# A two-layer decoder trunk: in the gated MLPs, the remainder of every second weight piece made by an accumulating transfer

## The chip, the cores and the metric

The kernel runs on one core of a Trainium2 chip, in one launch. Times are microseconds (us) on the device; the metric is the median of several runs. A separate execution was recorded by the hardware profiler, and all views quoted below come from it. The engines are called PE (TensorE; PEld is its weight load), DVE (VectorE), ACT (ScalarE), POOL (GpSimd) and SP (SyncE). SP issues the weight loads.

## The reference, cut to what matters

The input is a float32 residual stream of 256 tokens by 2048 features. Two layers follow. Each has a mixer (layer 0: gMLP beside HGRN2, layer 1: FoX attention) and then a gated MLP with a short causal convolution; the change concerns the MLP alone:

```
def conv_ffn(h, w_up, conv_w, conv_b, w_down):
    z = h @ w_up                                   # 2048 -> 2 * 5632
    zp = pad(z, two rows of zeros ahead)
    z = sum(conv_w[j] * zp[:, j:j + seq] for j in range(3)) + conv_b
    a, b = split(z, 2)
    return (silu(a) * b) @ w_down                  # 5632 -> 2048
...
x = x + conv_ffn(rms_norm(x, ffn_norm[l]), ...)
```

All weights are float32, and the products are wanted at nearly float32 precision.

## The kernel before, in words

**Layout.** The stream is kept feature-major: sixteen tiles `xT[m]` of 128 features by 256 tokens. A product with a weight matrix has the weights stationary in PE (128 x 128) and the tokens moving.

**Two-part products.** PE takes operands in a reduced form of float32 (`F32R`). To keep the precision, a value is split into a rounded part and the remainder. For activations, `split` puts the rounded part into columns 0 to 255 of a 128 x 512 tile and the remainder into columns 256 to 511. For weights, `weights(src, n)` loads a piece `w` (SP), lets ACT copy it to `wh` with rounding (L139), and lets DVE make the remainder `wl = w - wh` (L141).

**A projection.** `project` makes 128 output features from all input features. It takes its weights in two pieces: `chunks=(8, 8)`, two pieces of 128 x 1024 (512 KB each), in the up-projections, and `chunks=(6, 5)`, pieces of 128 x 768 (384 KB) and 128 x 640 (320 KB), in the down-projections. For each of the 16 or 11 input tiles there are two matmuls: `wh` against all 512 columns (L155) and `wl` against the first 256 (L157), both into one accumulator `pm`. That pair is called a pair below. `fold` (L187, L188) adds the two halves of the accumulator; `project_norm` then multiplies with the norm's factor R (L195); `add_x` (L264 to L266) adds the result of a down-projection to the stream.

**The MLP.** `ffn` handles the 44 hidden tiles in four groups of eleven. `up(g)` runs `conv` for the a and the b part of each tile: one up-projection, the convolution on ACT and DVE (L673 to L675), then silu, the product and the split into `hid`. `down(g)` runs sixteen down-projections over the group's eleven tiles. The order is up(0), up(1), down(0), up(2), down(1), up(3), down(2), down(3). In all, each layer's MLP has 88 up-projections and 64 down-projections, 88 x 16 + 64 x 11 = 2112 pairs of matmuls.

**Buffers and order.** Weight pieces come from two pools. `wp` lives for the whole kernel and has four buffers for `w`, three for `wh` and three for `wl`. A second pool, `fw`, is opened for each MLP (`deep["pool"]`) in memory that the mixer used before, and has four, two and two. `deep["turn"]` counts the pieces of an MLP: the first six come from `wp`, and from then on every second piece comes from `fw`. A framework plans the order of the instructions on each engine and sets all the waits; each engine then works through its own list in order. An instruction that fills a buffer waits until the last reader of the buffer's previous contents is done, so the number of buffers sets how far ACT, DVE and the loads may run ahead of PE.

**GpSimd** has almost nothing to do: one small load at the start and some additions in the first 30 us.

Of the kernel before, what the change touches and what calls it, by code (L numbers as in the profile page):

```python
# [7 lines left out]
F32 = mybir.dt.float32  # L8
F32R = mybir.dt.float32r
BF16 = mybir.dt.bfloat16  # L10
AF = mybir.ActivationFunctionType
ALU = mybir.AluOpType
AX = mybir.AxisListType

P = 128
# [7 lines left out]
GRP = 11  # L23
# [21 lines left out]
def tile_trunk(ctx: ExitStack, tc: tile.TileContext, x, pp_d, cst_d, mlev_d, msk_d,  # L45
               w_v, w_f, w_g, w_i, w_q, w_u, w_abo, w_cf, w_cqkv, w_cg, w_co, w_up, w_dn, spw_d, spb_d, out):
    nc = tc.nc
    V, SC, PE = nc.vector, nc.scalar, nc.tensor

    cp = ctx.enter_context(tc.tile_pool(name="cp", bufs=1))  # L50
    wp = ctx.enter_context(tc.tile_pool(name="wp", bufs=4))
# [7 lines left out]
    def nm(base):  # L59
        count[0] += 1  # L60
        return f"{base}_{count[0]}"
# [3 lines left out]
    for c0, n in ((0, 2), (2, 2), (4, 4), (8, 4), (12, 4)):  # L65
        t = cp.tile([P, n, S], F32, tag=f"x{c0}", name=f"x{c0}")
# [15 lines left out]
    def act(out_, in_, func, **kw):  # L82
        name = TABLE.get(func)
        if name is not None and name != epoch["set"]:
            ld = SC.preload_act_table_set(name)
            for o in epoch["ops"]:
                tc.add_manual_dep(ld.ins, o.ins.name, order, reason="table order")
            epoch.update(set=name, load=ld, ops=[ld])
        r = SC.activation(out_, in_, func, **kw)
        if name is not None:  # L90
            tc.add_manual_dep(r.ins, epoch["load"].ins.name, order, reason="table order")
            epoch["ops"].append(r)
        return r
# [14 lines left out]
    def tick():  # L108
        while queue and len(flight) < depth[0]:
            flight.append(queue.pop(0))  # L110
        for g in list(flight):
            if next(g, flight) is flight:
                flight.remove(g)
# [11 lines left out]
        while flight or queue:  # L125
            tick()

    deep = {"pool": None, "turn": 0}

    def weights(src, n):  # L130
        deep["turn"] += 1
        if deep["pool"] is not None and deep["turn"] > 6 and deep["turn"] % 2:
            pool, nw, ns = deep["pool"], 4, 2
        else:
            pool, nw, ns = wp, 4, 3
        w = pool.tile([P, n], F32, tag="w", name=nm("w"), bufs=nw)
        nc.sync.dma_start(w, src)
        wh = pool.tile([P, n], F32R, tag="wh", name=nm("wh"), bufs=ns)
        SC.activation(wh, w, AF.Copy)  # L139
        wl = pool.tile([P, n], F32R, tag="wl", name=nm("wl"), bufs=ns)  # L140
        V.tensor_tensor(wl, w, wh.bitcast(F32), ALU.subtract)  # L141
        return wh, wl

    def project(wsrc, acts, chunks=(8, 8), k0=0):
        ps = pm.tile([P, 512], F32, tag="pm", name=nm("pm"))
        nk = sum(chunks)
        done = 0
        for c in chunks:
            lo = (k0 + done) * P
            tick()  # L150
            wh, wl = weights(wsrc[:, lo:lo + c * P], c * P)
            for k in range(c):
                a = acts[done + k]
                first, last = done + k == 0, done + k == nk - 1
                PE.matmul(ps, wh[:, k * P:(k + 1) * P], a,  # L155
                          start=first, stop=False, skip_group_check=True)
                PE.matmul(ps[:, S:2 * S], wl[:, k * P:(k + 1) * P], a[:, 0:S],  # L157
                          start=False, stop=last, skip_group_check=True)
            done += c
        return ps  # L160
# [24 lines left out]
    def fold(ps):  # L185
        t = tp.tile([P, S], F32, tag="ev", name=nm("ev"), bufs=3)
        SC.activation(t, ps[:, S:2 * S], AF.Copy)  # L187
        V.tensor_tensor(t, ps[:, 0:S], t, ALU.add)  # L188
        return t

    def project_norm(wsrc, acts, R, out=None):
        t = fold(project(wsrc, acts))
        if out is None:
            out = t
        V.tensor_tensor(out, t, R, ALU.mult)  # L195
        return out

    def split(dst, src, gain=None):
        if gain is None:
            SC.activation(dst[:, 0:S], src, AF.Copy)  # L200
            V.tensor_tensor(dst[:, S:2 * S], src, dst[:, 0:S].bitcast(F32), ALU.subtract)
        else:
            SC.activation(dst[:, 0:S], src, AF.Copy, scale=gain)
            V.scalar_tensor_tensor(dst[:, S:2 * S], src, gain, dst[:, 0:S].bitcast(F32),  # L204
                                   ALU.mult, ALU.subtract)
# [56 lines left out]
    def add_x(m, ps):  # L262
        t = tp.tile([P, S], F32, tag="ev", name=nm("ev"), bufs=3)
        SC.activation(t, ps[:, S:2 * S], AF.Copy)  # L264
        V.tensor_tensor(xT[m], xT[m], ps[:, 0:S], ALU.add)
        V.tensor_tensor(xT[m], xT[m], t, ALU.add)  # L266

# [1 line left out]
    def mixer_ab(norm):  # L269
        es = ExitStack()  # L270
        hp = es.enter_context(tc.tile_pool(name="hp", bufs=1))
# [4 lines left out]
        def keep(n):  # L276
            return hp.tile([P, S], F32, tag="keep", name=nm(n), bufs=3 * NH)

        # gMLP's v, two groups of four heads with the tokens on the partitions
        gv, late = [], []  # L280

        def finish():
# [6 lines left out]
        for g in range(2):  # L289
            ps = project_tok(w_v[g], norm, feed=g == 0)  # L290
            v = hp.tile([P, 2, 512], F32, tag="tok", name=nm("gv"), bufs=2)
# [5 lines left out]
            else:  # L297
                drain()
                R, Rt = late
                for T in range(2):  # L300
                    act(v[:, T], ps[T], AF.Gelu, scale=Rt[:, T:T + 1])
        A = norm.a
# [18 lines left out]
        for g in range(2):  # L321
            for T in range(2):
                i = (2 * g + T) * 4
                j = hp.tile([P, 512], F32, tag="smk", name=nm("junk"), bufs=1)
# [28 lines left out]

        queue.append(mixes())

        # the lower bound, softmax over the first axis of gamma
        gam = pp[:, C_GAM:C_GAM + 3 * NH]
        gm = hp.tile([P, 4 * NH], F32, tag="gm", name="gm")
        mx, sm_, lb, omlb = (gm[:, i * NH:(i + 1) * NH] for i in range(4))
# [16 lines left out]
        for h in range(NH):  # L376
            z = project_norm(w_f[h], A, R)
            l = keep("lf")
            t = hp.tile([P, 2, S], F32, tag="two", name=nm("kq"), bufs=2 * NH)
# [101 lines left out]
        for h in range(NH):  # L481
            z = fold(project(w_q[h], A))
# [29 lines left out]
        for h in range(NH):  # L512
            z = hp.tile([P, S], F32, tag="zu", name=nm("zu"), bufs=5)
# [16 lines left out]
        for m in range(KT):  # L530
            add_x(m, project(w_abo[m], ks))
            nxt.feed(m)
        es.close()
        return nxt

# [1 line left out]
    def mixer_c(norm):  # L537
        es = ExitStack()
        hp = es.enter_context(tc.tile_pool(name="cpool", bufs=1))
# [112 lines left out]
        es.close()  # L652
        return nxt

# [1 line left out]
    def ffn(l, norm, last):  # L656
        es = ExitStack()
        hp = es.enter_context(tc.tile_pool(name="fp", bufs=1))
        deep.update(pool=es.enter_context(tc.tile_pool(name="fw", bufs=1)), turn=0)
        A = norm.a  # L660
        R = norm.finish()
        nxt = None if last else Norm(C_MIX + KT)

        def conv(j):
            z = project_norm(w_up[l, j], A, R)

            def w(i):
                c = C_CW + (l * 3 + i) * 2 * HT + j
                return pp[:, c:c + 1]

            cb = C_CB + l * 2 * HT + j
            c = hp.tile([P, S], F32, tag="conv", name=nm("conv"), bufs=4)
            SC.activation(c, z, AF.Identity, bias=pp[:, cb:cb + 1], scale=w(2))  # L673
            V.scalar_tensor_tensor(c[:, 1:], z[:, :S - 1], w(1), c[:, 1:], ALU.mult, ALU.add)  # L674
            V.scalar_tensor_tensor(c[:, 2:], z[:, :S - 2], w(0), c[:, 2:], ALU.mult, ALU.add)  # L675
            return c

        def up(g):
            hid = []
            for i in range(GRP):  # L680
                j = g * GRP + i
                a = conv(j)
                b = conv(HT + j)
                act(a, a, AF.Silu)
                V.tensor_tensor(a, a, b, ALU.mult)
                t = hp.tile([P, 512], F32R, tag="hid", name=nm("hid"), bufs=2 * GRP)
                split(t, a)
                hid.append(t)
            return hid

        def down(g, hid):
            for m in range(KT):
                add_x(m, project(w_dn[l, m], hid, chunks=(6, 5), k0=g * GRP))
                if g == HT // GRP - 1:
                    if last:
                        nc.sync.dma_start(out[:, m, :], xT[m])
                    else:
                        nxt.feed(m)

        hids = [up(0)]  # L700
        for g in range(HT // GRP):
            if g + 1 < HT // GRP:
                hids.append(up(g + 1))
            down(g, hids[g])
        deep["pool"] = None
        es.close()
        return nxt

    banks.update(px=3, pd=2)
    norm = mixer_ab(Norm(C_MIX))  # L710
    norm = ffn(0, norm, False)
    norm = mixer_c(norm)
    ffn(1, norm, True)


# [78 lines left out]
```

## Time and profile before

| | before |
|---|---|
| time, median of 3 runs | 2390.92 us |
| lowest and highest run | 2390.84 and 2404.64 us |
| span of the profiled execution | 2389.0 us |
| median minus span | 1.9 us |
| mean granted PE clock | 0.999 of full speed |
| PE / PEld busy | 2377.3 / 2060.0 us |
| DVE / ACT / POOL busy | 1756.3 / 1317.2 / 16.1 us |
| moved by DMA | 440.73 MB, mean 184 GB/s |
| first gated MLP | from about 429 to 1162 us |
| second gated MLP | from about 1640 us to the end |

The profiled execution's own time is its span, from the first to the last instruction, and what lies around it; the runs' median is 1.9 us above the span. A group of instructions is given as line, engine, operation, `out<-in` by the program's names, shapes and count, then busy time, mean nanoseconds of one, and the idle time of the engine just before, with what ended it. In the lists of waits, a row says who waited for whom, then the total in us, how often, and the longest. In windows, the columns are the length, the busy time of PE, PEld, DVE, ACT and POOL (with the number of instructions), the granted PE clock, the mean busy share of the 16 DMA engines, and GB/s. For DMA issues, KB is the size of one and the last number is the median time from issue to landing. PE's matmuls are pipelined and their ends are modelled, so a full PE is not a PE at its peak.

### The profile page before, as it was taken

The numbers are of one execution on the slowest core, as the hardware profiler recorded it, in microseconds if no ns is written. First come the engines' busy times: TensorE is split into PE (matmuls) and PEld (weight loads), VectorE is DVE, ScalarE is ACT, GpSimd is POOL, SyncE is SP. The second block draws the span as 40 slices with busy tenths as digits, with TensorE's granted clock in tenths as the row PEclk, the third lists the DMA queues.
The fourth block names the chain that finished last, engine by engine and source line by source line (L and its number), as shares of the span: only waits on it lengthen the run. The fifth ranks groups of instructions, "written<-read, shape, count | busy, mean of one in ns | idle before, by whom it ended". The sixth has DMA issues, their size and how long they took to land.

```text
span 2389.0 us, 35728 instructions
## 1 busy us (share of the span) xinstructions
PE 2377.3 (100%) x13198; PEld 2060.0 (86%) x13198; DVE 1756.3 (74%) x2954; ACT 1317.2 (55%) x2169; POOL 16.1 (1%) x20
## 2 busy tenths in 40 slices
PE   8999999999999999999999999999999999999999
PEld 7888888888888888888888888888888888888888
DVE  6767786888867877777756666777777767767765
ACT  6655565655555555555545455556555555545543
POOL 2000000000000000000000000000000000000000
PEclk9999999999999999999999999999999999999999
DMA  7544455755566566566655555557555565565564
GB/s 265 177 159 135 141 184 187 241 190 191 169 187 213 177 173 222 176 170 188 200 175 177 175 159 167 188 192 237 186 186 186 156 220 186 152 220 185 153 188 145
DMA packets 133869, 440.73 MB, mean 184 GB/s; under 512 B 14880, under 2 KB 16944, under 8 KB 133440
## 3 DMA queue, kind: packets, MB, share of 16 engines
q1 hardware_dynamic: 132224, 433.40, 57.5%
q10 hardware_dynamic: 1440, 5.01, 0.6%
q8 instruction: 104, 1.70, 0.3%
q14 instruction: 69, 0.57, 0.1%
q0 software_dynamic: 32, 0.05, 0.0%
HBM read 436.29 MB, written 2.11 MB: 184 GB/s over the span
## 4 chain that ended last, share of the span: by engine, by line
PE 97%; DMA 1%; DVE 1%; issue 0%; ACT 0%; SPq 0%; DVEq 0%; ACTq 0%
PE pm L155 53%; PE pm L157 27%; PE pm L177 5%; PE pm L178 5%; PE pm L176 5%; PE px L439 1%; DVE wl L141 0%; DMA w<-in_w_v 0%; DMA mst<-in_mlev 0%; PE pd L411 0%; DMA w<-in_w_up 0%; PE pd L412 0%; PE px L612 0%; PE px L576 0%; PE px L583 0%
## 5 line engine op out<-in xcount | busy, mean ns | idle before, releaser
L141 DVE TENSOR_TENSOR wl<-w,wh 128x1024 fp32r<-128x1024 f32 (+3 forms) x900 | 1015.7, 1129 | 538.1 <-ACT wh L139 534.3
L139 ACT ACTIVATE wh<-w 128x1024 fp32r<-128x1024 f32 (+3 forms) x900 | 883.4, 982 | 952.2 <-PE pm L155 653.4
L155 PE MATMUL pm<-a,wh 128*128 128x512 f32 x3600 | 1266.0, 396 | 0.0
L157 PE MATMUL pm<-a,wl 128*128 128x256 f32 x3600 | 1010.5, 281 | 0.5 <-DVE wl L141 0.5
L155 PEld LDWEIGHTS pm<-a,wh 128*128 128x128 f32 x3600 | 675.0, 187 | 157.1 <-DVE a L204 0.8
L157 PEld LDWEIGHTS pm<-a,wl 128*128 128x128 f32 x3600 | 680.3, 189 | 1.6 <-DVE wl L141 0.8
L155 PE MATMUL pm<-hid,wh 128*128 128x512 f32 x1408 | 493.1, 395 | 0.0
L157 PE MATMUL pm<-hid,wl 128*128 128x256 f32 x1408 | 394.8, 280 | 0.0
L155 PEld LDWEIGHTS pm<-hid,wh 128*128 128x128 f32 x1408 | 263.9, 187 | 61.9
L157 PEld LDWEIGHTS pm<-hid,wl 128*128 128x128 f32 x1408 | 266.0, 189 | 0.0
L176 PE MATMUL pm<-wh,a 128*128 128x512 f32 x512 | 204.0, 400 | 2.1 <-ACT wh L139 2.1
L177 PE MATMUL pm<-wl,a 128*128 128x512 f32 x512 | 202.0, 395 | 3.5 <-DVE wl L141 3.5
L178 PE MATMUL pm<-wh,a 128*128 128x512 f32 x512 | 201.6, 394 | 0.0
L177 PEld LDWEIGHTS pm<-wl,a 128*128 128x128 f32 x512 | 97.0, 189 | 25.3 <-DVE wl L141 5.9
L176 PEld LDWEIGHTS pm<-wh,a 128*128 128x128 f32 x512 | 97.2, 190 | 21.7 <-ACT wh L139 2.4
L178 PEld LDWEIGHTS pm<-wh,a 128*128 128x128 f32 x512 | 96.7, 189 | 20.2
L673 ACT ACTIVATE conv<-ev,pp 128x256 f32<-128x256 f32 x176 | 103.4, 587 | 16.2 <-DVE ev L195 16.2
L188 DVE TENSOR_TENSOR ev<-pm,ev 128x256 f32<-128x256 f32 x225 | 93.8, 417 | 3.4 <-ACT ev L187 3.4
L674 DVE SCALAR_TENSOR_TENSOR conv<-ev,pp,conv 128x255 f32<-128x255 f32 x176 | 84.2, 478 | 8.1 <-ACT conv L673 8.1
L675 DVE SCALAR_TENSOR_TENSOR conv<-ev,pp,conv 128x254 f32<-128x254 f32 x176 | 85.1, 483 | 6.2
L155 PE MATMUL pm<-yc,wh 128*128 128x512 f32 x256 | 88.8, 391 | 0.0
L195 DVE TENSOR_TENSOR ev<-ev,R 128x256 f32<-128x256 f32 x184 | 78.3, 425 | 6.1
(181 smaller groups left out, 1602.7 us busy)
## 6 DMA issues: line engine op xcount, KB each, us to landing
w<-in_w_up SPq DMA_DIRECT2D x352, 512.0 KB, 4.3
w<-in_w_dn SPq DMA_DIRECT2D x128, 384.0 KB, 3.2
w<-in_w_cqkv SPq DMA_DIRECT2D x96, 512.0 KB, 3.6
w<-in_w_dn SPq DMA_DIRECT2D x128, 320.0 KB, 3.3
w<-in_w_abo SPq DMA_DIRECT2D x32, 512.0 KB, 4.3
w<-in_w_cg SPq DMA_DIRECT2D x32, 512.0 KB, 3.9
w<-in_w_co SPq DMA_DIRECT2D x32, 512.0 KB, 3.5
w<-in_w_f SPq DMA_DIRECT2D x16, 512.0 KB, 3.6
```

The lines of the kernel that those rows point to most:

```text
L139: SC.activation(wh, w, AF.Copy)
L141: V.tensor_tensor(wl, w, wh.bitcast(F32), ALU.subtract)
L155: PE.matmul(ps, wh[:, k * P:(k + 1) * P], a, start=first, stop=False, skip_group_check=True)
L157: PE.matmul(ps[:, S:2 * S], wl[:, k * P:(k + 1) * P], a[:, 0:S], start=False, stop=last, skip_group_check=True)
L176: PE.matmul(ps[T], ah, h, start=k + i == 0, stop=False)
L177: PE.matmul(ps[T], ah, l, start=False, stop=False)
L178: PE.matmul(ps[T], al, h, start=False, stop=k + i == KT - 1)
L188: V.tensor_tensor(t, ps[:, 0:S], t, ALU.add)
L195: V.tensor_tensor(out, t, R, ALU.mult)
L673: SC.activation(c, z, AF.Identity, bias=pp[:, cb:cb + 1], scale=w(2))
L674: V.scalar_tensor_tensor(c[:, 1:], z[:, :S - 1], w(1), c[:, 1:], ALU.mult, ALU.add)
L675: V.scalar_tensor_tensor(c[:, 2:], z[:, :S - 2], w(0), c[:, 2:], ALU.mult, ALU.add)
```

## The change

A second way to make the two parts of a weight piece, `weights_acc`, is added. It loads `w` as before. ACT writes the negated, rounded copy of `w` straight into `wl`. GpSimd then issues a transfer from `w` to `wl` that adds to what is there, so that `wl` becomes `w` minus the rounded `w`. A second copy on ACT makes `wh` as before. DVE has no part in it. `project` gets an argument `acc`, the offsets of the pieces that go this way: the second piece of each up-projection (offset 8) and the second piece of each down-projection (offset 6). All pieces of the new kind come from the pool `fw`, now with four buffers for `w`, four for `wl` and three for `wh`, from the first projection of an MLP on; all others come from `wp`. The counter `turn` is gone. The mixers use `weights` as before.

```diff
-    deep = {"pool": None, "turn": 0}
+    deep = {"pool": None}
 
     def weights(src, n):
-        deep["turn"] += 1
-        if deep["pool"] is not None and deep["turn"] > 6 and deep["turn"] % 2:
-            pool, nw, ns = deep["pool"], 4, 2
-        else:
-            pool, nw, ns = wp, 4, 3
+        pool, nw, ns = wp, 4, 3
         w = pool.tile([P, n], F32, tag="w", name=nm("w"), bufs=nw)
         nc.sync.dma_start(w, src)
         wh = pool.tile([P, n], F32R, tag="wh", name=nm("wh"), bufs=ns)
...
+    def weights_acc(src, n):
+        pool = deep["pool"]
+        w = pool.tile([P, n], F32, tag="w", name=nm("w"), bufs=4)
+        nc.sync.dma_start(w, src)
+        wl = pool.tile([P, n], F32R, tag="wl", name=nm("wl"), bufs=4)
+        SC.activation(wl, w, AF.Copy, scale=-1.0)
+        nc.gpsimd.dma_start(wl, w, accum_op=ALU.add)
+        wh = pool.tile([P, n], F32R, tag="wh", name=nm("wh"), bufs=3)
+        SC.activation(wh, w, AF.Copy)
+        return wh, wl
+
-    def project(wsrc, acts, chunks=(8, 8), k0=0):
+    def project(wsrc, acts, chunks=(8, 8), k0=0, acc=()):
...
-            wh, wl = weights(wsrc[:, lo:lo + c * P], c * P)
+            wh, wl = (weights_acc if done in acc else weights)(wsrc[:, lo:lo + c * P], c * P)
...
-    def project_norm(wsrc, acts, R, out=None):
-        t = fold(project(wsrc, acts))
+    def project_norm(wsrc, acts, R, out=None, acc=()):
+        t = fold(project(wsrc, acts, acc=acc))
...
-        deep.update(pool=es.enter_context(tc.tile_pool(name="fw", bufs=1)), turn=0)
+        deep.update(pool=es.enter_context(tc.tile_pool(name="fw", bufs=1)))
...
-            z = project_norm(w_up[l, j], A, R)
+            z = project_norm(w_up[l, j], A, R, acc=(8,))
...
-                add_x(m, project(w_dn[l, m], hid, chunks=(6, 5), k0=g * GRP))
+                add_x(m, project(w_dn[l, m], hid, chunks=(6, 5), k0=g * GRP, acc=(6,)))
```

## The prediction

> **What bounds the kernel now.** The profile page comes first: the engines' shares and the chain that ended last.
>
> ```profile
> span 2389.0 us, 35728 instructions
> ...
> PE 2377.3 (100%) x13198; PEld 2060.0 (86%) x13198; DVE 1756.3 (74%) x2954; ACT 1317.2 (55%) x2169; POOL 16.1 (1%) x20
> ...
> q1 hardware_dynamic: 132224, 433.40, 57.5%
> ...
> PE 97%; DMA 1%; DVE 1%; issue 0%; ACT 0%; SPq 0%; DVEq 0%; ACTq 0%
> ```
>
> TensorE is busy for 2377.3 of 2389.0 us, so all idle time of PE together is 11.7 us, and the chain is 97% PE. VectorE's 74% and the DMA queue's 57.5% lie beside it. The waits say whether VectorE, which the change relieves, ever holds PE up.
>
> ```profile
> ACT wh L139 <- PE pm L155: 653.4, 573, 3.1
> DVE wl L141 <- ACT wh L139: 534.3, 752, 3.5
> ...
> PEld pm L177 <- DVE wl L141: 5.9, 6, 2.5
> ...
> PE pm L177 <- DVE wl L141: 3.5, 4, 2.1
> ...
> PEld pm L157 <- DVE wl L141: 0.8, 1, 0.8
> ```
>
> It hardly does. L177 is in the token-major projections of the mixers, which the change leaves alone; L157, the matmul on `wl` that the gated MLPs use, has 0.8 us in one wait. The long waits run the other way: ScalarE waits for PE to give a `wh` buffer back, 653.4 us in 573 waits, 1.14 us each. ScalarE and VectorE are ahead of PE and stop because the buffers are full. Last, the two gated MLPs as windows (columns: PE, weight load, DVE, ACT, POOL busy, clock, DMA share, GB/s).
>
> ```profile
> 429.00:1162.00 733.00, 733.00 (x4228) 645.99 (x4228) 566.97 (x909) 414.84 (x669) 0.00 (x0) 1.00 0.61 189
> 1640.00:2389.00 749.00, 744.33 (x4210) 644.73 (x4208) 553.67 (x876) 399.65 (x634) 0.00 (x0) 1.00 0.59 184
> ```
>
> These two stages are 1482 us of the span. In the first PE is never idle, in the second for 4.67 us. So VectorE's relief has at most 4.67 us to give here; the question is only whether what replaces its work stays below PE.
>
> **The change part by part.** Per layer there are 88 up-projections of two 1024-wide pieces and 64 down-projections of a 768- and a 640-wide piece. The second piece of each takes the new way: 88 + 64 = 152 pieces per layer, 304 in all. Their prices by shape, first gated MLP:
>
> ```profile
> L141 DVE TENSOR_TENSOR wl<-w,wh 128x1024 fp32r<-128x1024 f32 x176 | 215.5, 1225 | 86.2 <-ACT wh L139 85.8
> ...
> L139 ACT ACTIVATE wh<-w 128x1024 fp32r<-128x1024 f32 x177 | 187.7, 1062 | 195.1 <-PE pm L155 191.8 <-DMA w<-in_w_up 1.5 <-issue 1.4
> ...
> L141 DVE TENSOR_TENSOR wl<-w,wh 128x640 fp32r<-128x640 f32 x64 | 52.7, 824 | 31.7 <-ACT wh L139 31.7
> ...
> L139 ACT ACTIVATE wh<-w 128x640 fp32r<-128x640 f32 x64 | 47.3, 739 | 42.5 <-PE pm L155 41.0
> ```
>
> *Removed:* 88 subtractions of 1.225 us and 64 of 0.824 us, 107.8 + 52.7 = 160.5 us of VectorE per layer, 567 down to 406. All of it lay beside PE: gain 0, at most the 4.67 us above.
>
> *Added on ScalarE:* the negated copy, a second ACTIVATE of the same shape: 88 x 1.062 + 64 x 0.739 = 93.5 + 47.3 = 140.8 us per layer, 414.8 up to 555.6 of 733 us (76%). It is hidden by the idle time in which ScalarE now waits for PE. If that cover were gone, it would cost at most those 140.8 us per layer. The new copy waits for its `w` and for one of four `wl` buffers, and behind it in ScalarE's order stand the `wh` copies of the next pieces and the copy L187 that empties the accumulators; for these PE waits. The buffers reach about three projections ahead, so I take 0.
>
> *Added on GpSimd:* 304 transfers. The trace has one DMA issue by POOL, and POOL does nothing else in these stages:
>
> ```profile
> 1.24 0.68 POOL L74 DMA_DIRECT2D pp<-in_pp  x1 [0.79 <-POOLq L783]
> ...
> pp<-in_pp POOLq DMA_DIRECT2D x1, 50.0 KB, 6.3
> ```
>
> At 0.68 us per issue 88 + 64 issues are 103 us per layer: POOL is no bound, even at double that. In its order each transfer waits for the negated copy, with only later transfers queued behind it, all for later pieces. Landing takes 4.3 us in the median for a load of 512 KB (row below), and a transfer of twice the work some 9 us. `wl` has four buffers in every second piece, so a transfer may start three projections ahead: PE takes 733 us for 152 projections, 4.8 us each, so some 14 us. The delay of one transfer is hidden; what counts is how much all of them take of the DMA engines.
>
> *Added on the 16 DMA engines, the main term.* A transfer takes 512 KB (up) or 320 KB (down) of `w` and adds it onto the `wl` of that size: 88 x 0.524 + 64 x 0.328 = 67.1 MB per layer for one pass. The trace shows no accumulating transfer and none from SBUF to SBUF; the nearest rows are the weight loads.
>
> ```profile
> 426.00:429.00 3.00, 3.00 (x17) 2.33 (x16) 1.96 (x3) 1.53 (x4) 0.00 (x0) 1.00 1.00 362
> 429.00:432.00 3.00, 3.00 (x18) 2.66 (x18) 2.05 (x4) 2.59 (x5) 0.00 (x0) 1.00 1.01 380
> 435.00:438.00 3.00, 3.00 (x19) 2.63 (x18) 2.96 (x4) 2.87 (x5) 0.00 (x0) 1.00 1.01 377
> 444.00:447.00 3.00, 3.00 (x19) 2.63 (x19) 2.55 (x5) 1.89 (x5) 0.00 (x0) 1.00 1.00 384
> ...
> w<-in_w_up SPq DMA_DIRECT2D x352, 512.0 KB, 4.3
> ```
>
> Two prices follow. On average over a stage: 0.61 x 733 us for 189 GB/s x 733 us = 138.5 MB, 3.23 us of all 16 engines per MB (second stage 0.59 x 749 / 137.8 = 3.21). In bursts, with all 16 engines full: mean of 362, 380, 377 and 384 is 376 GB/s, 2.66 us per MB. The difference is that a packet's time has waiting in it, which overlaps with the next packet's once the queues are full.
>
> Bounds for the transfers: at best one pass at the burst price, 67.1 x 2.66 = 178 us per layer; at worst three passes (read `w`, read `wl`, write `wl`, nothing overlapped) at the average price, 201.3 x 3.23 = 650 us. Less than nothing is excluded, since all the loads stay. I take two passes, since both operands must be read while writing can run beside it, at the average price, since reading back what will be written is a less even stream than a load: 134.2 x 3.23 = 433 us (second layer 134.2 x 3.21 = 431). It is close to the middle of the ends, 414. The loads then run with full queues, at the burst price: 138.5 x 2.66 = 368 us (137.8 x 2.66 = 367). Sums: 801 us of DMA against 733 us of PE in the first MLP, 798 against 749 in the second. The DMA engines become the bound: +68 and +49, together +117 us. VectorE, ScalarE and PE then wait; what is late is `wl` of the second piece, and through the `w` buffers the loads.
>
> The Trainium skill, Collectives: The Full Stack, "The bandwidth ceiling: the fold count and why AG ≠ RS ≠ AR", says that an addition made by the DMA engines costs nothing for itself, but reads two sources over one ring and so runs at half the rate of a copy: the two passes I count. No run here shows it yet. DMA: Bandwidth & Descriptors, "Issuing engines are not separate DMA queues", speaks against the change as well: a transfer from GpSimd runs on the same 16 DMA engines as the loads from SyncE.
>
> *Moved: the start of each MLP.* Now the first six pieces come from `wp`, already free; after the change the second piece of the first projection needs the MLP's own pool, whose memory the mixer held.
>
> ```profile
> 408.39 0.33 SPq L137 DMA_DIRECT2D w<-in_w_up  x1
> ...
> 422.39 0.84 SPq L137 DMA_DIRECT2D w<-in_w_up  x2
> ...
> 428.86 2.01 ACT L139 ACTIVATE wh<-w 128x1024 fp32r<-128x1024 f32 x2 [1.47 <-DMA w<-in_w_up]
> ...
> 1639.87 7.59 DMA w<-in_w_up
> 1647.49 1.07 ACT wh L139
> ...
> 1651.43 1.23 DVE wl L141
> 1652.71 0.39 PE pm L157
> ```
>
> SyncE issues the MLP's loads one by one from 408.39, and in pairs from 422.39, which I read as the new pool's memory coming free. Such a load is there at about 428.9. Then come the negated copy 1.06, the issue 0.68 and the landing 4.3 to 9: `wl` at 435 to 440. PE is through with the first piece at about 429.4 + 2.8 = 432.2 (8 pairs at 733 / 2112 = 0.347 us): a stall of 3 to 7 us. In the second layer the chain already has such a stall (load until 1647.46, PE on at 1652.71); 1647.5 + 1.1 + 0.7 + 4.3 to 9 = 1653.6 to 1658.3, 1 to 6 us more. I take +8 for both together.
>
> **The sum.** 0 (VectorE) + 0 (ScalarE, POOL) + 117 (DMA engines) + 8 (starts) = +125 us. The profiled execution has a span of 2389.0 us; the runs' median is 2390.92, 1.9 more, which lies around the span. 2390.9 + 125 = 2516 us, 5% slower. The case's own range runs from 2415, the 1% line, to 2700.
>
> **The rivals.**
>
> *A. The transfers stay hidden.* Two passes at the burst price: 134.2 x 2.66 = 357, with the loads 725 us, below 733 and 749. For it: the queues would be full, and in such stretches the rows show 376 GB/s. Against it: that is 99% of the first stage, with no room for a less even stream. Only the starts are left: 2390.9 + 8 = 2399 us. It decides at 365 / 134.2 = 2.72 us per MB: below that PE stays the bound. If the 4.67 us of idle time also went, 2386. By the Trainium skill, DMA: Bandwidth & Descriptors, "Where 436 GB/s comes from", traffic within SBUF is bound by 435 GB/s and not by HBM; its two passes would be 309 us by an estimate from that figure, and the sum 677 us, so this rival; no run here shows it.
>
> *B. The accumulating stream is much slower than a copy.* Three passes at the average price: 650 + 368 = 1018 us (+285) and 646 + 367 = 1013 (+264): 2390.9 + 549 + 8 = 2948 us. For it: the nearest rows show loads only, and a read-add-write cannot start writing before both reads are back. Against it: 16 engines work on 128 rows at once. Stalls could also lower the clock: the row with 0.55 us of PE in 2 us is followed by 0.51; the shorter gaps of 18 to 20 us keep 1.00.
>
> ```profile
> 6.00:8.00 2.00, 0.55 (x3) 0.25 (x2) 0.37 (x3) 0.43 (x2) 0.00 (x0) 1.00 1.04 406
> ...
> 10.00:12.00 2.00, 2.00 (x7) 1.51 (x6) 1.69 (x3) 1.48 (x5) 0.93 (x1) 0.51 1.03 388
> ...
> 18.00:20.00 2.00, 1.43 (x7) 0.89 (x6) 2.00 (x3) 2.00 (x5) 1.92 (x2) 1.00 0.63 225
> ```
>
> *C. ScalarE becomes the bound.* If each of the 304 negated copies brought a wait of 1.14 us that nothing absorbs, 347 us: 2738 us. Against it: such waits shrink as soon as PE is late, and 733 - 555.6 = 177 us of idle time per layer would take up 152 x 1.14 = 173.
>
> *D. Faster.* The second MLP has fewer matmul records in 40 us than the first:
>
> ```profile
> 500.00:540.00 40.00, 40.00 (x233) 35.28 (x232) 32.07 (x50) 22.36 (x35) 0.00 (x0) 1.00 0.58 191
> ...
> 1780.00:1820.00 40.00, 40.00 (x228) 34.67 (x227) 31.92 (x51) 22.74 (x36) 0.00 (x0) 1.00 0.56 185
> ```
>
> If the new placing of the buffers gave it the first one's pace, 749 would become 733 and the whole 2375, still within 1%. Nothing says that it would.
>
> **How the numbers follow.** The forecast (DMA-bound, 2415 to 2700) 0.46; B and other prices above 2700 0.20; C 0.04; A, with D's part within 1%, 0.27; faster by over 1% 0.03. One per cent, some 24 us, is about what a measurement of this kernel can tell from no change. So slower 0.46 + 0.20 + 0.04 = 0.70, same 0.27, faster 0.03. The range goes from 2386 (A with its gain) to 2750, above C; beyond it lies the larger part of B.
>
> **What would show it.** Right: in the changed profile the DMA share of both MLPs is over 0.9, `q0 software_dynamic` holds some 134 MB or more, PE waits for DMA `wl` at L157 and its busy share falls to about 95%, ScalarE's waits for PE shrink, and the mixers' stages keep their lengths. Each MLP would be about 800 us long. Wrong: a DMA share below 0.9 with PE still full (A); MLPs of 1000 us (B); PE waiting for `wh` from ScalarE with DMA engines idle (C).

## The result, and the profile after

With the change the kernel takes 2407.62 us in the median of 20 runs, against 2391.39 us before: 16.2 us more. The ratio is 1.0056, 95% interval [1.003, 1.0082]. That is a small loss, not the 5% forecast; rival A (hidden transfers, 2399 us) was the case that happened. One thing has to be known to read the numbers: the times of each of these two kernels fall into three groups some 14 us apart (before: about 2377, 2391 and 2405; after: about 2394, 2408 and 2422), and the groups of the two kernels are all about 17 us apart.

The page of the changed kernel, same parts as before:

```profile
span 2404.7 us, 36262 instructions
...
PE 2380.0 (99%) x13198; PEld 2061.4 (86%) x13198; DVE 1469.7 (61%) x2650; ACT 1581.1 (66%) x2473; POOL 274.9 (11%) x324
...
q1 hardware_dynamic: 132224, 433.40, 52.3%
q0 software_dynamic: 43808, 134.29, 30.0%
...
w<-in_w_up SPq DMA_DIRECT2D x352, 512.0 KB, 8.6
wl<-w POOLq DMA_DIRECT2D x176, 512.0 KB, 8.3
```

VectorE lost 287 us of work, ScalarE gained 264, and PE's busy time is nearly what it was (2380.0 against 2377.3). The DMA engines move 134 MB more, and loads and transfers of 512 KB alike take over 8 us to land; the loads took 4.3 before. The windows of the two gated MLPs (columns as before):

```profile
429.00:1180.00 751.00, 745.66 (x4208) 645.55 (x4207) 423.70 (x756) 546.14 (x818) 129.32 (x152) 1.00 1.00 273
...
1655.00:2405.00 750.00, 739.49 (x4251) 650.57 (x4249) 414.02 (x732) 532.78 (x791) 129.36 (x152) 1.00 0.99 275
```

The DMA share is 1.00 and 0.99, up from 0.61 and 0.59, and still PE is nearly full. A share of 1.00 is thus not the sign of a bound. PE's waits over the whole span say the same:

```profile
PEld pm L164 <- DMA wl<-w: 12.4, 4, 5.3
PE pm L164 <- DMA wl<-w: 10.9, 4, 4.9
```

Only four matmuls waited for a transfer (the wait shows at the matmul and at its weight load). All four stand at the starts of the MLPs, two in each (start, duration; in brackets the idle time before and what ended it):

```profile
437.70 0.39 PE L164 MATMUL pm<-a,wl 128*128 128x256 f32 x1 [4.24 <-DMA wl<-w]
451.56 0.39 PE L164 MATMUL pm<-a,wl 128*128 128x256 f32 x1 [0.97 <-DMA wl<-w]
...
1673.52 0.50 PE L164 MATMUL pm<-a,wl 128*128 128x256 f32 x1 [4.85 <-DMA wl<-w]
1687.20 0.39 PE L164 MATMUL pm<-a,wl 128*128 128x256 f32 x1 [0.84 <-DMA wl<-w]
```

Windows of 4 us at the first start show what they cost. A matmul that crosses a border counts in both windows; a full window shows 25.

```profile
428.00:432.00 4.00, 3.87 (x20) 2.89 (x19) 1.88 (x4) 3.62 (x6) 1.07 (x2) 1.00 1.03 353
432.00:436.00 4.00, 1.46 (x8) 0.92 (x6) 1.28 (x3) 3.97 (x5) 0.94 (x2) 1.00 1.04 255
436.00:440.00 4.00, 2.30 (x8) 2.01 (x9) 0.00 (x0) 0.38 (x1) 0.57 (x1) 0.75 1.08 207
440.00:444.00 4.00, 4.00 (x20) 3.44 (x20) 0.85 (x2) 1.88 (x3) 0.26 (x1) 0.82 0.89 267
444.00:448.00 4.00, 4.00 (x24) 3.48 (x24) 3.08 (x6) 4.00 (x8) 1.24 (x2) 1.00 1.01 315
448.00:452.00 4.00, 3.03 (x17) 2.42 (x16) 3.38 (x8) 4.00 (x7) 0.20 (x1) 1.00 1.05 215
452.00:456.00 4.00, 4.00 (x24) 3.47 (x23) 1.63 (x5) 2.69 (x5) 0.84 (x1) 1.00 0.87 179
```

The same stretch as one window, then the second start, and after them the same two places in the kernel of experiment 1 below, which has no stall there:

```profile
428.00:456.00 28.00, 22.66 (x116) 18.63 (x115) 12.10 (x26) 20.54 (x30) 5.11 (x6) 0.94 1.00 256
1664.00:1692.00 28.00, 22.24 (x115) 18.55 (x114) 11.98 (x26) 20.27 (x29) 5.10 (x6) 0.94 0.99 251
```

```profile
428.00:456.00 28.00, 28.00 (x161) 24.36 (x161) 20.68 (x36) 25.10 (x37) 4.43 (x6) 1.00 1.03 292
1644.00:1672.00 28.00, 28.00 (x162) 24.37 (x160) 20.18 (x36) 24.68 (x37) 4.24 (x5) 1.00 1.02 307
```

At 28 / 161 = 0.174 us a matmul, the first start lost 45 x 0.174 = 7.8 us and the second 47 x 0.173 = 8.1 us. Together that is 15.9 us, about the measured difference. (The slower pace of the change's first MLP, told in the last section, can be at most 0.6 us of the 7.8.) The four waits are 10.9 us of it. More than half of the other 5 us went in the windows with a lower granted clock (0.75 and 0.82 at the first start), which follow the long waits: from 437.9 to 441.4 us PE's pairs of matmuls start 0.64 us apart instead of 0.35.

The stall at 448 us is a consequence of the first. ScalarE and GpSimd at that place (columns as in the list of waiting matmuls):

```profile
435.34 1.04 ACT L148 ACTIVATE wh<-w 128x1024 fp32r<-128x1024 f32 x1
442.12 0.39 ACT L194 ACTIVATE ev<-pm 128x256 f32<-128x256 f32 x1 [5.74 <-PE pm L164]
442.40 1.05 ACT L145 ACTIVATE wl<-w 128x1024 fp32r<-128x1024 f32 x1
...
429.92 0.88 POOL L146 DMA_DIRECT2D wl<-w  x1 [399.67 <-DMA w<-in_w_up]
431.81 0.86 POOL L146 DMA_DIRECT2D wl<-w  x1 [1.01 <-ACT R L89]
435.73 0.85 POOL L146 DMA_DIRECT2D wl<-w  x1 [3.06 <-ACT wl L145]
443.74 0.84 POOL L146 DMA_DIRECT2D wl<-w  x1 [7.17 <-ACT wl L145]
```

ScalarE's next instruction in order was the copy that empties an accumulator (L194), and PE was late with that. The negated copy behind it could only run at 442.40, so the fourth transfer was issued at 443.74, 8 us after the third, and landed at 451.5, just too late again.

### The profile page after: what moved, and what is told of

It is laid out like the page before. It is cut to its first block, busy times and chain, and to the rows that moved or that the text cites. A ratio compares the mean times of both kernels' runs of the same rounds, so it can differ in the third digit from the quotient of the medians.

```text
span 2404.7 us, 36262 instructions
## 1 busy us (share of the span) xinstructions
PE 2380.0 (99%) x13198; PEld 2061.4 (86%) x13198; DVE 1469.7 (61%) x2650; ACT 1581.1 (66%) x2473; POOL 274.9 (11%) x324
## 4 chain that ended last, share of the span: by engine, by line
PE 95%; DMA 2%; issue 1%; DVE 1%; ACT 0%; POOL 0%; SPq 0%; POOLq 0%; DVEq 0%; ACTq 0%
PE pm L162 52%; PE pm L164 27%; PE pm L184 4%; PE pm L185 4%; PE pm L183 4%; DMA wl<-w 1%; PE px L446 1%; DVE wl L137 0%; DMA w<-in_w_up 0%; DMA mst<-in_mlev 0%; PE pd L418 0%; PE pd L419 0%; DMA kst<-in_msk 0%; PE px L619 0%; PE px L583 0%
## 5 line engine op out<-in xcount | busy, mean ns | idle before, releaser
L164 PE MATMUL pm<-a,wl 128*128 128x256 f32 x3600 | 1011.5, 281 | 12.2 <-DMA wl<-w 10.9
L137 DVE TENSOR_TENSOR wl<-w,wh 128x1024 fp32r<-128x1024 f32 (+2 forms) x596 | 694.2, 1165 | 347.1 <-ACT wh L135 345.3
L135 ACT ACTIVATE wh<-w 128x1024 fp32r<-128x1024 f32 (+2 forms) x596 | 600.6, 1008 | 375.5 <-PE pm L185 137.8
L146 POOL DMA_DIRECT2D wl<-w x304 | 258.7, 851 | 2098.8 <-ACT wl L145 1091.8
L148 ACT ACTIVATE wh<-w 128x1024 fp32r<-128x1024 f32 (+1 forms) x304 | 280.7, 923 | 228.5 <-PE pm L162 228.2
L145 ACT ACTIVATE wl<-w 128x1024 fp32r<-128x1024 f32 (+1 forms) x304 | 278.6, 916 | 47.3 <-DMA w<-in_w_up 47.0
L272 DVE TENSOR_TENSOR x<-x,pm 128x256 f32<-128x256 f32 x160 | 67.1, 419 | 114.0 <-ACT ev L271 113.4
```

The costliest lines, as they stand in the source:

```text
L145: SC.activation(wl, w, AF.Copy, scale=-1.0)
L146: nc.gpsimd.dma_start(wl, w, accum_op=ALU.add)
```

## The experiments

**1. No transfers in the first three projections of each MLP.**

```diff
+        made = [0]
+
         def conv(j):
-            z = project_norm(w_up[l, j], A, R, acc=(8,))
+            made[0] += 1
+            z = project_norm(w_up[l, j], A, R, acc=(8,) if made[0] > 3 else ())
```

> The first three projections of each MLP take both pieces from wp with the VectorE subtraction; all later ones are as in the change. Theory 1 (the loss sits at the two starts: wl of the second piece comes 7 to 10 us after its issue, PE stops, ScalarE then stands behind the copy that empties the accumulator): PE's idle time at the starts goes back to before's 0 and 4.7 us, and the median to 2391 to 2396 us. Theory 2 (full DMA queues slow PE all along): the steady stretches hold the loss, so 2404 to 2408 us as with the whole change.

Measured: 2391.45 us, ratio to before 1.0001 [0.9964, 1.0037], median to median 16 us below the change. 298 of the 304 transfers are still there. Two long windows, one inside each MLP, and one 4 us window of the first start:

```profile
480.00:1160.00 680.00, 680.00 (x3925) 599.56 (x3924) 391.99 (x700) 499.05 (x756) 118.04 (x139) 1.00 1.00 277
1700.00:2360.00 660.00, 660.00 (x3810) 581.94 (x3809) 369.79 (x651) 476.78 (x710) 116.91 (x138) 1.00 1.01 280
...
436.00:440.00 4.00, 4.00 (x25) 3.51 (x24) 3.65 (x8) 4.00 (x7) 0.86 (x1) 1.00 1.03 295
```

PE is never idle there, at a DMA share of 1.00, and runs its 25 matmuls in the place where the change had 8. So theory 1 holds in its main point: the transfers cost nothing in the steady part, and the whole loss is at the starts. Theory 2 falls.

**2. The first projection only.** As experiment 1 with `made[0] > 1`.

> As the run that kept the first three projections of each MLP off the transfers, but only the first one of each MLP is kept off. If the loss at the starts is the landing time of the first transfer against the 2.8 us of PE work ahead of it, one projection more of cover (5.5 us, 8.3 in all) leaves a stall of at most 2 us at each start: 2391 to 2396 us. If the loss came from the full queues of the first 20 us as such, about 2400 us or more would be left.

Measured: 2407.98 us, ratio 1.0068 [1.0036, 1.0101]. That is no better than the change, so the expectation of a small rest was wrong; but the loss is one long stall at each start and not a slower pace: PE waits 5.16 us at the first and 4.94 us at the second. The profiled execution has a span of 2390.1 us, 11.7 us more than that of experiment 1, with PE equally fast in the MLPs of both (the same 233 matmuls in 40 us). The chain of waits and the windows of the first start:

```profile
429.26 8.67 DMA wl<-w
437.98 0.58 PE pm L164
...
428.00:432.00 4.00, 4.00 (x23) 3.18 (x22) 2.26 (x6) 3.98 (x8) 1.73 (x2) 1.00 0.98 266
432.00:436.00 4.00, 0.82 (x5) 0.46 (x3) 2.83 (x7) 3.52 (x4) 0.01 (x1) 0.86 1.02 284
436.00:440.00 4.00, 2.02 (x6) 1.80 (x7) 0.79 (x1) 0.00 (x0) 0.00 (x0) 0.50 0.91 207
440.00:444.00 4.00, 4.00 (x20) 3.44 (x19) 0.85 (x2) 1.47 (x3) 0.00 (x0) 0.79 0.95 343
```

The cover was counted wrongly. The order of PE's instructions shows that nearly all of the first projection stands between the mixer's last matmuls, so that it is done by 430 us; after that PE had only the first piece of the second projection, 2.8 us, before it needed the first transfer's `wl`. The transfer was issued at 429.26, as early as in the change, and took 8.67 us. In experiment 1 the first transfer is issued at 429.93, but four more pieces stand ahead of its use. Two projections kept off were not tried.

**3. The same pools and buffers, without a transfer.** `wl` is again made by VectorE, in the new pool.

```diff
-        SC.activation(wl, w, AF.Copy, scale=-1.0)
-        nc.gpsimd.dma_start(wl, w, accum_op=ALU.add)
         wh = pool.tile([P, n], F32R, tag="wh", name=nm("wh"), bufs=3)
         SC.activation(wh, w, AF.Copy)
+        V.tensor_tensor(wl, w, wh.bitcast(F32), ALU.subtract)
```

> The pools, buffers and order of the change, but wl in them made by the VectorE subtraction from wh: no transfer, no negated copy. Theory 1 (the transfer's landing makes the stall at the starts): PE idle at the first start under 2 us, median 2391 to 2395 us. Theory 3 (the second piece's memory, held by the mixer, makes it, whatever makes wl): PE idle at the starts as with the change, some 4 to 5 us each, and 2400 us or more.

Measured: 2395.77 us, ratio 1.0016 [0.9982, 1.005], 0.8 us above theory 1's range. PE's idle time is 0.17 us at the first start and 0.02 us at the second. The late memory of the pool does not make the stall alone: theory 3 falls. The transfer's own way, from the negated copy to the landing, has to be there; whether it would stall PE with early memory too was not tried.

**4. Transfers in the down-projections only.** `conv` calls `project_norm` without `acc`.

> Only the down-projections use the transfers (128 of 304, 21.0 of 67.1 MB per layer); every up-projection takes both pieces from wp. Theory 1 (starts): no transfer stands at a start, so 2391 to 2394 us. Theory 2 (full queues slow PE in proportion to the bytes): 21.0 / 67.1 of 16 us, so 2396 us; the DMA share should be over 0.9 in the down stretches only.

Measured: 2391.98 us, ratio 1.0002 [0.9969, 1.0035]. The DMA share was 1.02 in a down stretch (880 to 930 us) and 0.55 in an up stretch (480 to 640 us), with PE full in both. This speaks for theory 1 too, though 2396 us, theory 2's figure, lies inside the interval; experiment 1 decides. One thing was not as expected: transfers do stand at the start. Four of them, for pieces that PE needs only in down(0), are issued from 428.97 to 440.55 us, and SyncE issues no load of an up-projection between 428.94 and 436.96, since loads for such pieces stand in its order. ScalarE then waits 5.36 us for a load, until 445.62, and PE is idle for 1.6 us between 446 and 452. Whether that order or the full DMA queues made the load late was not tried apart.

**5. The prices by themselves.** A kernel with five stages of 48 rounds each and no computation, in which only the eight buffers limit how many transfers are under way.

```diff
+    # loads from HBM
+    for i in range(N):
+        load(i)
...
+    # copies within SBUF, from SP
+    for i in range(N):
+        nc.sync.dma_start(dst[i % NB].bitcast(F32), src[i % 2])
...
+    # copies within SBUF, from GpSimd
+    for i in range(N):
+        nc.gpsimd.dma_start(dst[i % NB].bitcast(F32), src[i % 2])
...
+    # accumulating transfers
+    for i in range(N):
+        nc.gpsimd.dma_start(dst[i % NB], src[i % 2], accum_op=ALU.add)
...
+    # two loads to each accumulating transfer
+    for i in range(N):
+        load(2 * i)
+        load(2 * i + 1)
+        nc.gpsimd.dma_start(dst[i % NB], src[i % 2], accum_op=ALU.add)
```

> Nothing of the model is computed; the input is copied out. Five stages, kept apart by barriers, each with 48 rounds of 128x1024 float32 (0.524 MB) over eight buffers: loads from HBM by SP; copies within SBUF by SP; copies within SBUF by GpSimd; accumulating transfers within SBUF by GpSimd; two loads by SP to each accumulating transfer. Price of the forecast: 1.39 us for each load (2.66 us per MB), 3.4 us for each accumulating transfer (two passes at 3.23), 6.2 us for two loads and a transfer. Rival A: 2.8 us (two passes at 2.66) or less, 5.5 us together. If the second read costs nothing on the DMA engines, a transfer takes 1.4 us or less, and two loads and a transfer about 4.2 us.

One execution was measured. Windows of the five stages in this order (columns: length, DVE, ACT, POOL, clock, DMA share, GB/s):

```profile
21.00:82.00 61.00, 7.22 (x47) 0.00 (x0) 0.00 (x0) 1.00 1.01 401
86.00:143.00 57.00, 0.00 (x0) 0.00 (x0) 0.00 (x0) 1.00 1.02 407
150.00:208.00 58.00, 0.00 (x0) 0.00 (x0) 22.36 (x43) 1.00 1.02 389
...
230.00:330.00 100.00, 0.00 (x0) 0.00 (x0) 31.01 (x36) 1.00 1.06 199
...
352.00:515.00 163.00, 6.61 (x43) 0.00 (x0) 35.06 (x41) 1.00 1.06 275
```

Loads run at 401 GB/s, copies within SBUF at 389 to 407, and accumulating transfers at 199: half. So a transfer of 512 KB (0.524 MB) takes 0.524 / 0.199 = 2.63 us of all 16 engines, two passes at 2.51 us per MB. That lies below rival A's 2.8 us and well below the 3.4 us of the forecast. GpSimd is busy for only 31 of the 100 us, so issuing is not the limit. Beside loads it is the same. The transfers ran ahead of the loads there, so the window has about one load to a transfer and not two. Its 41 transfers issued in 163 us are 132 GB/s, which leaves 143 GB/s of loads, 143 / 401 = 36% of the engines, and 132 GB/s in the other 64% are a rate of 205 GB/s.

With these prices the sum of the prediction becomes 138.4 / 0.401 + 67.1 / 0.199 = 345 + 337 = 682 us per MLP, 93% of 733.

**6. More transfers: both pieces of every up-projection.** `acc=(0, 8)` in `conv`.

> As the change, but both pieces of every up-projection are made by the transfers (480 transfers instead of 304, 113.3 MB per layer instead of 67.1). The DMA engines must now be the bound. By the measured prices (loads at 401 GB/s, transfers at 200 GB/s) an MLP takes 138.4 / 0.401 + 113.3 / 0.200 = 345 + 567 = 912 us, and the whole 2391 + (912 - 733) + (912 - 749) = 2733 us, some 20 more for the starts. By the forecast's prices an MLP takes 368 + 2 x 113.3 x 3.23 = 1100 us and the whole about 3110 us. If the 273 GB/s at a DMA share of 1.00 in the change were the limit, an MLP would take (138.4 + 113.3) / 0.273 = 922 us, which this run cannot tell from the first.

Measured: 2842.16 us in one run, span 2840.4. Its two MLPs, and inside the first a stretch of up-projections and one of down-projections:

```profile
429.00:1395.00 966.00, 805.69 (x4257) 665.33 (x4258) 328.13 (x671) 619.80 (x908) 203.16 (x240) 0.98 1.02 261
1875.00:2840.00 965.00, 801.04 (x4226) 662.52 (x4226) 310.75 (x633) 604.87 (x872) 203.80 (x240) 0.97 1.02 261
...
500.00:540.00 40.00, 30.84 (x157) 24.95 (x156) 11.64 (x26) 26.29 (x38) 9.34 (x11) 0.96 1.04 261
1300.00:1340.00 40.00, 40.00 (x229) 34.74 (x228) 19.58 (x34) 27.17 (x47) 8.49 (x10) 1.00 1.03 283
```

Now the DMA engines are the bound, in the up stretches alone. The expectation averaged over the MLP and came out at 912 us; the measured 965 us are above that, since the stretches cannot lend to each other. Worked out by stretch, after the run, an up-projection costs 1.049 / 0.401 + 1.049 / 0.199 = 7.9 us of DMA, 694 us for 88, and a down-projection stays at PE's 3.8 us, 244 us for 64: 938 us, 3% below what was measured. (The up stretch above shows 157 matmuls in 40 us, 8.2 us for a projection's 32.) The forecast's prices gave 1100. Both stretches have a DMA share over 1.0, and only one of them waits. The change itself has to be taken by stretch too: an up-projection costs 1.049 / 0.401 + 0.524 / 0.199 = 5.25 us of DMA against 16 x 0.347 = 5.55 us of PE, a down-projection 0.721 / 0.401 + 0.328 / 0.199 = 3.45 against 3.82. So the transfers fit in both, in the up stretches with 5% to spare.

**7. Each transfer twice**, the second time onto one of three spare tiles. (Four would have needed 60 KB per partition for the pool, where 56.84 were free.)

```diff
         nc.gpsimd.dma_start(wl, w, accum_op=ALU.add)
+        spare = deep["spare"][deep["n"] % 3]
+        deep["n"] += 1
+        nc.gpsimd.dma_start(spare[:, 0:n], w, accum_op=ALU.add)
...
```

> As the change, but each transfer is issued a second time, onto one of three spare tiles that nothing reads: 134.2 MB more of transfers in all. Per MLP, with the loads at 368 us: by the forecast's price (two passes at 3.23 us per MB) 368 + 867 = 1235, in all about 3390 us; by rival A's (two passes at 2.66) 368 + 714 = 1082, about 3080 us; if a transfer costs one pass at 2.66, 368 + 357 = 725, hidden, about 2410 us. Three spare tiles also mean that a second transfer waits until the third before it has landed, which alone would allow one every 3 us or so.

Measured: 3138.66 us in one run; the second MLP lasted 1107 us, from 2030 to 3137. By the measured prices, 88 x 7.9 + 64 x (0.721 / 0.401 + 0.655 / 0.199) = 694 + 326 = 1020 us. The run is 9% above that, 2% above rival A's 1082 and 10% below the forecast's 1235. The three spare tiles, which the expectation named as a limit of their own, may make the rest, or PE's granted clock of 0.89 in this MLP; neither was tried apart.

## Why the prediction was wrong

**What held.** *VectorE's relief is worth nothing:* its work in the first MLP fell from 567 to 424 us (406 forecast) and PE gained nothing. *ScalarE hides the negated copy in the steady part:* 546 us against the 555.6 worked out. *GpSimd is no bound:* 0.85 us per issue instead of the 0.68 taken, 129 us per MLP. *Transfers reach far enough ahead:* no wait in the steady part, at 8.3 us to land.

**The step that failed: the price of the transfers in the main term.** That a transfer costs two passes was right: 199 GB/s against 389 to 407 for plain copies within SBUF is a factor of 1.95 to 2.05. The Trainium skill, Collectives: The Full Stack, "The bandwidth ceiling: the fold count and why AG ≠ RS ≠ AR", states for ReduceScatter that an addition on the way reads two sources and so runs at half the rate of a copy. The transfers of this case agree in the rate; no run here shows the two reads themselves. What was wrong is the price of a pass, 3.23 us per MB, taken from the share of a stage that was only 61% busy. It measured 2.51. The loads were also a little too dear, 2.66 against 2.49. So 433 + 368 = 801 us was really 337 + 345 = 682, and the sign of the main term turned, since PE's 733 us lie between the two. The prediction had seen that a MB is cheaper when the engines are full (2.66 against 3.23). It used the full price for the loads and not for the transfers, although both were to run with full queues.

**The range was hit without the mechanism.** The measured 2407.6 us lies inside 2386 to 2750 because the range took in rival A, and not because the DMA engines became the bound.

**The sign to look for was wrong as well.** A DMA share over 0.9 was named as proof of the forecast, and a share below 0.9 as the mark of rival A. The share rose to 1.00 in the case of rival A.

**The starts were the right mechanism, and too small.** +8 was forecast; about 16 was measured. The first wait at each start was well placed: 4.24 and 4.85 us, inside the forecast's 3 to 7 and 1 to 6. It left out two things: the second stall by way of ScalarE's order (0.97 and 0.84 us), and the lower clock after a long one. In the change the granted clock was 0.75 and 0.82 in the two windows after the wait of 4.24 us; in experiment 2 it was 0.50 in the window in which the wait of 5.16 us ended. After the wait of 0.97 us it stayed at 1.00. The Trainium skill, TensorE: Matmul & The Clock Gate, "Part 1: The HAM clock gate (the "warmup" mystery)", says that an idle window of about 3.4 us brings the clock down to half. The trace agrees with these waits: pairs 0.64 us apart instead of 0.35 after the one of 4.24 us, and 0.50 after that of 5.16.

**One reading was off, without effect on the sum.** The "stall" that the prediction saw in the second layer before the change was small: PE waited 0.51 us for VectorE's `wl` before its matmul at 1652.71. The rest of the 4.67 us of idle time lies after PE's last matmul.

**D came true by chance.** The paces of the two MLPs changed places: 228 matmul records in 40 us in the first and 233 in the second (rows at the end), the reverse of before. It brought nothing, since each profile has one MLP of each pace. That the new placing of the buffers does it is not shown: by the rows at the end, experiment 1, with the pools of the change, has the quicker pace in both MLPs.

## What to carry to other kernels

Price a transfer by what the DMA engines move when they are full, taken from a stretch or a small kernel that fills them, never by the busy share of a half-loaded stage; and count an accumulating transfer at twice its bytes. Add up by stretch: a stretch that is over its limit cannot borrow from one that is under it. Work that is hidden in the steady part can still cost at the start of a stage, where its landing time stands against the little work ahead of it: keep the slow path out of the first pieces. Relieving an engine that nobody waits for is worth nothing, even where it takes a quarter of that engine's work away.

## What the runs showed of the hardware that was not expected

An accumulating transfer within SBUF beside full loads leaves both at their own prices; no extra loss by the mixture was seen (205 GB/s beside loads, 199 alone).

PE has two paces for the same list of matmuls, some 2% apart, with a granted clock of 1.00 in both. Windows of 40 us in the first and the second MLP, of the change and then of experiment 1:

```profile
600.00:640.00 40.00, 40.00 (x228) 34.67 (x228) 23.69 (x43) 30.13 (x43) 5.95 (x7) 1.00 1.02 283
1780.00:1820.00 40.00, 40.00 (x233) 35.24 (x232) 24.65 (x45) 30.94 (x45) 5.98 (x7) 1.00 1.03 293
```

```profile
600.00:640.00 40.00, 40.00 (x233) 35.24 (x232) 24.23 (x44) 30.34 (x44) 5.95 (x7) 1.00 1.03 291
1780.00:1820.00 40.00, 40.00 (x232) 35.27 (x231) 23.79 (x43) 30.57 (x43) 5.96 (x7) 1.00 1.03 284
```

Experiment 1 has the quicker pace in both MLPs, and a span of 2378.4 us; the change, as the kernel before, has each pace in one of them. In the six profiles of the kernel before, the change and experiments 1 to 4, a pace holds through a whole MLP and changes only about its start or in a mixer. Some 2% of 733 us fit the 14 us between the groups of times, as if none, one or two MLPs ran at the slower pace; that is an argument from the sizes and was not shown. What chooses the pace stays open; it was not tried.
